# A fused two-block transformer kernel: the shared expert in plain fp32, all 64 experts routed, a new order of units

## The chip, the core and the metric

The kernel runs on one core of one Trainium2 chip. The metric is the device time of one execution in microseconds. A core has five engines with an instruction queue each: TensorE (PE, matmuls; its weight loads are listed as PEld), VectorE (DVE), ScalarE (ACT), GpSimd (POOL) and SyncE (SP). SP computes nothing here; its queue issues nearly all transfers from HBM. Each queue is executed in order, so an instruction that waits holds back all behind it on that engine.

## What is computed

Two blocks over 256 tokens of width 1024, in fp32. The change is in the mixture of experts of the first block:

```python
def moe_ffn(h, router_w, router_bias, w_gate, w_up, w_down, sh_gate, sh_up, sh_down):
    scores = jax.nn.sigmoid(hf @ router_w)               # 256 x 64
    # top 2 of each group of 8 -> best 4 of 8 groups -> best 8 experts of a token
    gate = gate / jnp.sum(gate, axis=-1, keepdims=True) * ROUTED_SCALE
    ...
    def expert_block(xb, e):
        return (jax.nn.silu(xb @ w_gate[e]) * (xb @ w_up[e])) @ w_down[e]
    routed = ...   # sum over each token's 8 experts, times its gate
    shared = (jax.nn.silu(hf @ sh_gate) * (hf @ sh_up)) @ sh_down
    return routed + shared
```

Every expert has three matrices of 1024 x 256 fp32 (gate, up, down), 1 MiB each. All 64 experts are read, whatever the tokens choose.

## The kernel before

The program runs six stages one after the other: the mixer of the first block (`first_mixer`), `moe`, and four stages of the second block. Weights come through one class, `Weights`: a plan lists all loads of the program in the order of use, `issue` puts a load on SP's queue whenever a buffer of 1 MiB is free, `next` hands out the next one and frees those used before. There are four buffers of tag `w`; a stage may lend more through `extra` (tags `a8`, `h2`). Weights marked for it are split into a high and a low fp32r part, `wh` by ACT (line 218) and `wl` by DVE or POOL (line 224), and then multiplied in three fp32r matmuls for each chunk (lines 289 to 291, or 325 to 327). Unmarked ones are used as they are, in plain fp32.

`moe` first normalises the mixer's output into `xn`, transposes it into `h_f` (`transpose_mod`) and splits that into `h_hi` and `h_lo`. The router (`router`, a generator) is interleaved with matmuls: each `yield from wait(W1)` and so on lets so many calls of `fast` pass, which stand between other matmuls. It scores the tokens, selects eight experts each, counts the tokens of each expert, ranks the experts by count, and writes the expert numbers by rank to `K.ids` (`r_ids`). Only then can SP load an expert's weights, since the address of a load (`rank_ap`) comes from `r_ids`; up to then SP can load only what does not depend on the routing.

Two sets of weights don't: the shared expert (item `("s",)`) and, as expert 0 is computed for all tokens without being ranked (`N_STATIC = 1`, item `("e", 0)`), that expert. Both are computed from split weights. The other 63 are taken by rank. The two busiest are computed for all 256 tokens ("dense", 3 loads). The others are packed into units of 128 token slots: one expert of 128 slots, 96 + 32, 64 + 64, or four of 32 (3, 6, 6 and 12 loads). A unit gathers its tokens (line 1481; one gather serves two units), multiplies gate and up (line 1500), is transposed, multiplies down (line 1531) and scatters the result into four PSUM banks (line 1543). `ORDER` is a table written by hand that sets the order of units and dense experts, and with it the order of loads: a unit's gate and up loads, then the down loads of the unit ahead of it.

If an expert has more tokens than its slots, `fallback` (line 1696) recomputes what is missing in a loop over all 64 experts. Its branch stands after item 1 and is passed by all engines; after it SP waits until all transfers issued so far have landed (line 1700), since both ways of the branch meet there.

Of the kernel before, what the change touches and what calls it, by code (L numbers as in the profile page):

```python
# [16 lines left out]
P = 128  # L17
# [456 lines left out]
def transpose_mod(K, xn, scale, shift, name, mid):  # L474
    nc = K.nc
    full = a8(K, name + "_f", tag="hf", bufs=1)
    hi, lo = a8r(K, name, tag="h2", bufs=2)
# [66 lines left out]
def plan_mix(I):  # L544
# [35 lines left out]
    for j in range(4):  # L580
# [4 lines left out]
W1, W2, W3, W4 = 13, 3, 3, 4  # L585
N_STATIC = 1
N_DENSE = 2
WHOLE, MIXED, HALVES, QUARTERS = (128,), (96, 32), (64, 64), (32,) * 4
DENSE = "dense"
ORDER = [WHOLE, HALVES, QUARTERS, MIXED, DENSE, QUARTERS, HALVES, DENSE, HALVES, MIXED, QUARTERS, WHOLE, HALVES,  # L590
         HALVES, QUARTERS, MIXED, QUARTERS, HALVES, HALVES, MIXED, QUARTERS, HALVES, HALVES, MIXED, QUARTERS, HALVES,
         WHOLE]
# [14 lines left out]
def _items():  # L607
    units = [Unit(o) for o in ORDER if o != DENSE]
# [7 lines left out]
    assert len(caps) == N_EXP - N_STATIC  # L616
# [8 lines left out]
    out = [("s",)] + [("e", e) for e in range(N_STATIC)]  # L625
# [17 lines left out]
def plan_moe(I):  # L643
    pl = []
    wg, wu, wd = I["w_gate"][0], I["w_up"][0], I["w_down"][0]

    def dense(gate, up, down):
        for w in (gate, up):
            pl.append((one(w.rearrange("(p k) f -> p k f", k=KC), (KC, D_EXP)), True))
        return [(one(down.rearrange("(k p) d -> p k d", p=P), (2, D)), lambda K: K.g2)]  # L650
# [12 lines left out]

    pend = []
    for it in ITEMS:
        if it[0] == "d":
            pl.extend(rows(w, it[1]) for w in (wg, wu))
        elif it[0] == "u":
            pl.extend(rows(w, r) for w in (wg, wu) for r in it[1].ranks)
        else:  # L670
            ws = [I[f"sh_{n}"][0] for n in ("gate", "up", "down")] if it[0] == "s" else [w[it[1]] for w in (wg, wu, wd)]
            nxt = dense(*ws)
        pl.extend(pend)
        if it[0] == "d":
            pend = [down(it[1])]
        elif it[0] == "u":
            pend = [down(r) for r in it[1].ranks]
        else:
            pend = nxt
    pl.extend(pend)  # L680
    return pl
# [429 lines left out]
def first_mixer(K, x, _):  # L1111
# [185 lines left out]
    inv_std(K, K.mo[1])  # L1297
# [3 lines left out]
def router(K, h_full, rw, rb, M):  # L1301
# [58 lines left out]
    nc.vector.scalar_tensor_tensor(ec[:, 2:3], ec[:, 1:2], M.kmul, M.kadd, op0=OP.mult, op1=OP.add)  # L1360
    nc.vector.reciprocal(tot, tot)
    for tt in range(TT):
        nc.vector.tensor_scalar(s[:, tt], s[:, tt], tot[:, tt:tt + 1], 2.5, op0=OP.mult, op1=OP.mult)
# [10 lines left out]
    pt = psum(K)  # L1374
    for i, src in enumerate((sel, s)):
        for tt in range(TT):
            nc.tensor.transpose(pt[:N_EXP, i * T + tt * P:i * T + tt * P + P], src[:, tt], K.ident)
# [6 lines left out]
    nc.vector.tensor_copy(K.ids, pi[0:1, :N_EXP])  # L1384
    nc.vector.tensor_copy(sg.rearrange("p a b -> p (a b)"), pt[:N_EXP])
# [9 lines left out]
    nc.vector.tensor_scalar(M.flag, om, 0.0, None, op0=OP.is_gt)  # L1395
    yield from wait(W4)
# [39 lines left out]
def dense_split(K, a, bufs=1):  # L1436
# [3 lines left out]
    return tuple(q.rearrange("p (a b) -> p a b", a=2) for q in (ah, al))  # L1440

# [105 lines left out]
def moe(K, x, _):  # L1547
# [8 lines left out]
    xn = a8(K, "xn", (TT, D))  # L1556
# [35 lines left out]
    K.W.flush()

    def mid(hf):
        if K.fast is None:
            K.fast = router(K, hf, rw, rb, M)
        fast(K)

    hh, hl, hf = transpose_mod(K, xn, K.mod[:, 3], K.mod[:, 2], "h2", mid)
    for tt in range(TT):  # L1600
        nc.scalar.activation(M.xn[0][:, tt], xn[:, tt], AF.Copy)
    g2 = K.g2 = wk.tile([P, D], F32, name="g2b", bufs=1)
    mod_bcast(K, K.mrow, 5, g2)
    K.W.extra = [("a8", 4, 4)]
    K.pool_sub = 1
    outs = [psum(K) for _ in range(4)]
    prev = scat = ahead = None
    for n, it in enumerate(ITEMS + [None]):
# [9 lines left out]
        else:  # L1618
            h = hf if it[0] == "d" else (hh, hl)
            pg = dense_proj(K, h)  # L1620
        if it == ("e", 0):
            for _ in K.fast:
                pass
            K.fast = None
            for tt in range(TT):
                nc.vector.tensor_sub(M.xn[1][:, tt], xn[:, tt], f32(M.xn[0][:, tt]))
            K.pool_sub = 3
        if prev is not None:
# [3 lines left out]
            else:  # L1632
                if pit[0] == "e":
                    dense_gate(K, act, (K.ident[:N_EXP, pit[1]:pit[1] + 1], M.sg[:, 1]))
                elif pit[0] == "d":
                    dense_gate(K, act, (M.perm[:, pit[1]:pit[1] + 1], M.sg[:, 1]))
                act = act.rearrange("p (a b) -> p a b", a=2) if pit[0] == "d" else dense_split(K, act)
# [3 lines left out]
        if n + 1 < len(ITEMS) and ITEMS[n + 1][0] == "u" and ITEMS[n + 1][2] == 0:  # L1641
            G = wk.tile([P, TT, T], F32R, name="u_G")
            pair = ITEMS[n + 1][3]
            sel = [unit_sel(K, u, M, G, P * q) for q, u in enumerate(pair)]
            xg_next = gather(K, G, M, P * len(pair))
            ahead = [unit_route(K, gg) for gg in sel], xg_next
# [5 lines left out]
        else:  # L1652
            cur = (it, dense_act(K, pg, dense_proj(K, h)))
        if it == ("e", 0):
            for tt in range(TT):
                nc.scalar.activation(x[:, tt], x[:, tt], AF.Copy, scale=ALPHA)
# [1055 lines left out]
```

## Time and profile before

| what | value |
|---|---|
| median of 3 runs (lowest to highest) | 1844.7 us (1844.55 to 1847.16) |
| the profiled execution: its time, its span | 1845.26 us, 1843.4 us |
| mean granted clock of TensorE | 0.977 |
| PE, DVE, ACT, POOL busy | 1710.4, 1001.1, 741.7, 450.3 us |
| read from HBM over the span | 400.04 MB |
| PE, share of the chain that ended last | 45% |
| DMA, share of that chain | 10% |

The profile is of one execution, in microseconds from the span's start. Busy shares are means over stages with different limits; the stage that the change touches lies between about 460 and 1035 us. A plain fp32 matmul shows as two records in the trace, so `x32` there are 16 matmuls of the program.

### The profile page before, as it was taken

How to read it: one execution, taken by the hardware profiler on the slowest of the kernel's cores; microseconds unless marked ns; L12 is line 12 of the kernel's file. 1: busy time of each engine (PE TensorE's matmuls, PEld its weight loads, DVE VectorE, ACT ScalarE, POOL GpSimd, SP SyncE). 2: the span in 40 equal slices, each digit the busy share in tenths (PEclk: the TensorE clock that was granted, in tenths of full speed). 3: DMA queues.
4: the chain of work that ended last, by engine and by line, in shares of the span. 5: the costliest groups of instructions: out<-in, count | busy, mean ns of one | idle time of the engine just before them, and what ended most of it. 6: DMA issues, size and time to landing. Idle time of an engine off the chain costs nothing.

```text
span 1843.4 us, 35420 instructions
## 1 busy us (share of the span) xinstructions
PE 1710.4 (93%) x14701; PEld 1397.0 (76%) x14701; DVE 1001.1 (54%) x1744; ACT 741.7 (40%) x1263; POOL 450.3 (24%) x331
## 2 busy tenths in 40 slices
PE   7999999998789999988898899999988889989999
PEld 5999988897674665544454588899978877779998
DVE  4764666557742223323332576744479967864444
ACT  3554666544421111211121354544447555544443
POOL 2232332224600110000000223223335533332222
PEclk9999999999799999999999999999999999999999
DMA  9666666554358998999999544465524300026552
GB/s 312 206 193 219 216 206 201 181 181 162 127 228 354 380 384 345 421 420 420 420 421 420 171 137 138 139 206 193 180 84 160 121 24 3 25 93 205 177 189 92
DMA packets 182711, 403.40 MB, mean 219 GB/s; under 512 B 12352, under 2 KB 140716, under 8 KB 155796
## 3 DMA queue, kind: packets, MB, share of 16 engines
q1 hardware_dynamic: 181700, 398.73, 59.6%
q8 instruction: 116, 1.90, 0.4%
q0 software_dynamic: 848, 2.38, 0.4%
q14 instruction: 47, 0.39, 0.1%
HBM read 400.04 MB, written 1.05 MB: 218 GB/s over the span
## 4 chain that ended last, share of the span: by engine, by line
PE 45%; DMA 10%; DVE 9%; issue 3%; ACT 2%; POOL 1%; SPq 0%; DVEq 0%; ACTq 0%; POOLq 0%
PE ps L1500 6%; DMA w<-in_w_gate_dram 5%; PE ps L290 5%; PE ps L289 5%; PE ps L291 5%; PE ps L1531 3%; DMA w<-in_w_down_dram 3%; PE ps L325 3%; PE ps L327 3%; PE ps L326 3%; PE ps L1481 2%; DMA w<-in_w_up_dram 2%; PE ps L1413 2%; DVE tmx L2123 1%; DVE wl L224 1%
## 5 line engine op out<-in xcount | busy, mean ns | idle before, releaser
L224 DVE TENSOR_TENSOR wl<-w,wh 128x1024 fp32r<-128x1024 f32 x220 | 334.3, 1533 | 179.0 <-ACT wh L218 178.6
L289 PE MATMUL ps<-hT_hi,wh 128*128 128x256 f32 (+1 forms) x1488 | 428.3, 288 | 0.0
L291 PE MATMUL ps<-hT_hi,wl 128*128 128x256 f32 (+1 forms) x1488 | 421.4, 283 | 1.9 <-POOL wl L224 1.1
L290 PE MATMUL ps<-hT_lo,wh 128*128 128x256 f32 (+1 forms) x1488 | 422.1, 284 | 1.0 <-DVE hT_lo L465 1.0
L224 POOL TENSOR_TENSOR wl<-w,wh 128x1024 fp32r<-128x1024 f32 x112 | 280.3, 2504 | 555.7 <-ACT wh L218 547.6
L218 ACT ACTIVATE wh<-w 128x1024 fp32r<-128x1024 f32 (+1 forms) x332 | 340.6, 1050 | 144.7 <-PE ps L290 96.1
L289 PEld LDWEIGHTS ps<-hT_hi,wh 128*128 128x128 f32 (+1 forms) x1488 | 284.6, 191 | 6.3 <-issue 3.8
L290 PEld LDWEIGHTS ps<-hT_lo,wh 128*128 128x128 f32 (+1 forms) x1488 | 284.8, 191 | 4.3 <-DVE hT_lo L465 3.0
L291 PEld LDWEIGHTS ps<-hT_hi,wl 128*128 128x128 f32 (+1 forms) x1488 | 284.7, 191 | 2.6 <-POOL wl L224 1.5
L1500 PE MATMUL ps<-w,xg 128*32 128x256 f32 (+2 forms) x2272 | 201.7, 393 | 24.0 <-DMA w<-in_w_gate_dram 12.8
L1500 PEld LDWEIGHTS ps<-w,xg 128*32 128x32 f32 (+2 forms) x2272 | 114.6, 124 | 113.9 <-issue 24.3
L1531 PE MATMUL ps<-w,u_aT 128*32 128x512 f32 (+2 forms) x568 | 103.1, 608 | 7.3 <-DMA w<-in_w_down_dram 7.2
L1507 ACT ACTIVATE u_s<-ps 128x256 f32<-128x256 f32 x25 | 9.6, 383 | 182.5 <-PE ps L1500 182.5
L1490 ACT ACTIVATE xg<-ps,modc 128x256 f32<-128x256 f32 (+1 forms) x52 | 28.9, 556 | 129.7 <-PE ps L1481 129.7
L1034 POOL DMA_DIRECT2D lngb<-in_ln_g_dram x2 | 1.3, 636 | 326.0 <-PE ps L1481 326.0
L499 ACT ACTIVATE u_yh<-res_t 128x512 fp32r<-128x512 f32 x50 | 31.5, 630 | 122.0 <-DVE res_t L1534 122.0
L1531 PEld LDWEIGHTS ps<-w,u_aT 128*32 128x32 f32 (+2 forms) x568 | 29.7, 122 | 66.2 <-issue 46.3
L1508 DVE SCALAR_TENSOR_TENSOR u_s<-u_s,u_gate,ps 128x256 f32<-128x256 f32 x25 | 12.0, 481 | 124.7 <-ACT u_s L1507 124.7
L325 PE MATMUL ps<-wh,e_ah 128*128 128x512 f32 x192 | 75.2, 392 | 0.0
L326 PE MATMUL ps<-wl,e_ah 128*128 128x512 f32 x192 | 75.2, 391 | 0.0
L327 PE MATMUL ps<-wh,e_al 128*128 128x512 f32 x192 | 74.8, 390 | 0.0
L1481 PE MATMUL ps<-u_G,xn_hi 128*128 128x256 f32 (+1 forms) x208 | 55.8, 304 | 12.6 <-DVE u_G L1451 12.6
(600 smaller groups left out, 3267.0 us busy)
## 6 DMA issues: line engine op xcount, KB each, us to landing
w<-in_w_gate_dram SPq DMA_DIRECT2D x64, 1024.0 KB, 16.6
w<-in_w_up_dram SPq DMA_DIRECT2D x64, 1024.0 KB, 14.0
w<-in_w_down_dram SPq DMA_DIRECT2D x64, 1024.0 KB, 15.7
w<-in_w_in_dram SPq DMA_DIRECT2D x36, 1024.0 KB, 5.3
w<-in_ffn_w_gate_dram SPq DMA_DIRECT2D x22, 1024.0 KB, 5.4
w<-in_ffn_w_up_dram SPq DMA_DIRECT2D x22, 1024.0 KB, 5.3
w<-in_ffn_w_down_dram SPq DMA_DIRECT2D x22, 1024.0 KB, 4.8
w<-in_w_ada_dram SPq DMA_DIRECT2D x16, 1024.0 KB, 7.8
```

Of the source, the lines that this page charges most:

```text
L218: nc.scalar.activation(h[:rows, :n], v, AF.Copy)
L224: eng.tensor_sub(l[:rows, :n], v, f32(h[:rows, :n]))
L289: mm(out, wh, xh[:, kc], start=kc == 0, stop=False)
L290: mm(out, wh, xl[:, kc], start=False, stop=False)
L291: mm(out, wl, xh[:, kc], start=False, stop=kc == nk - 1)
L325: mm(o, xh[:, xk + kc, ts], wh, start=first and kc == 0, stop=False)
L326: mm(o, xh[:, xk + kc, ts], wl, start=False, stop=False)
L327: mm(o, xl[:, xk + kc, ts], wh, start=False, stop=last and kc == nk - 1)
L1413: K.nc.tensor.matmul(o[:, i * T:i * T + T], w[1][0][:, kc, i::2], h[:, kc], start=kc == 0, stop=kc == KC - 1)
L1481: nc.tensor.matmul(o, src[:, tt, kc * P:kc * P + P], G[:, tt, :n], start=tt + i == 0, stop=tt + i == 2)
L1500: K.nc.tensor.matmul(gu[c:c + m, cs], xg[kc // 4][:, kc % 4, off + c:off + c + m], ts[j][:, kc], start=kc == 0, stop=kc == KC - 1, tile_po ...
L1531: nc.tensor.matmul(y[c0:c0 + m], aT[:, c, c0:c0 + m], ts[j][:, c, hf * 512:hf * 512 + 512], start=c == 0, stop=c == 1, tile_position=(0, c0))
```

## The change

The shared expert's weights are no longer split, nor is `h_f`; it is computed in plain fp32, its down weights are multiplied by `g2` on POOL ahead of the router (`dense_scale`), and the router's steps are placed between its matmuls. Expert 0 is ranked as the other 63. Two buffers of tag `h2` are lent from the start of the stage, and all ten from the end of the router. The first half of `xn` is written by DVE, no longer by ACT. `ORDER` is new: 25 units and two dense experts as before, one unit of 64 + 32 + 32 slots in place of one of 64 + 64, four experts first and last. The branch of `fallback` stands after the first unit.

```diff
-W1, W2, W3, W4 = 13, 3, 3, 4
-N_STATIC = 1
+W1, W2, W3, W4 = 18, 4, 3, 6
 N_DENSE = 2
-ORDER = [WHOLE, HALVES, QUARTERS, MIXED, DENSE, QUARTERS, HALVES, DENSE, HALVES, MIXED, QUARTERS, WHOLE, HALVES,
+KINDS = {"W": (128,), "M": (96, 32), "H": (64, 64), "T": (64, 32, 32), "Q": (32,) * 4}
+ORDER = "QWHMHQWWQHTHHQMHdQHdQMMMHHQ"
...
+    for nm in ("gate", "up"):
+        pl.append((one(I[f"sh_{nm}"][0].rearrange("(p k) f -> p k f", k=KC), (KC, D_EXP)), False))
+    pl.append((one(I["sh_down"][0].rearrange("(p k) d -> p k d", k=2), (2, D)), False))
...
-    for kc in range(KC):
-        nc.scalar.activation(hi[:, kc], full[:, kc], AF.Copy)
-        (nc.gpsimd if kc in (2, 4, 6, 7) else nc.vector).tensor_sub(lo[:, kc], full[:, kc], f32(hi[:, kc]))
-        if kc in (1, 5, 7):
-            mid(full)
-    return hi, lo, full
+    return full
...
             K.nc.tensor.matmul(o[:, i * T:i * T + T], w[1][0][:, kc, i::2], h[:, kc],
                                start=kc == 0, stop=kc == KC - 1)
+            fast(K)
...
+def dense_scale(K, w):
+    for c in range(2):
+        K.nc.gpsimd.tensor_mul(w[:, c], w[:, c], K.g2)
...
+    K.W.extra = [("a8", 3, 4), ("h2", 2, 2)]
+    K.W.issue()
+    mod_bcast(K, K.mrow, 5, g2)
...
+    nc.vector.tensor_scalar(xk[:, 0], xs[:, 0], mo[3], mo[4], op0=OP.mult, op1=OP.add)
+    inv_std(K, mo)
+    dense_scale(K, K.W.raw[K.W.i + 2][1][0])
...
+    hf = transpose_mod(K, xn, K.mod[:, 3], K.mod[:, 2], "h2")
+    K.fast = router(K, hf, rw, rb, M)
+    for _ in range(3):
+        fast(K)
...
+    act = dense_act(K, dense_proj(K, hf), dense_proj(K, hf))
+    for _ in K.fast:
+        pass
+    K.W.extra = [("a8", 4, 4), ("h2", 2, 2)]
+    dense_down(K, outs, K.W.next()[1][0], act, True)
+    ahead = route(ITEMS[0][3])
...
-        if n == N_STATIC:
+        if n == 0:
             fallback(K, x, hf, g2, M)
-            K.W.extra = [("a8", 4, 4), ("h2", 2, 2)]
```

PE's queue from the router's scores on, before: after scores (`rw`), `id` and a broadcast come split matmuls of the shared expert (`wh`, `wl`), 39 of them ahead of the counts (`ones<-r_br`); the ids are the rows of `r_pm`. The first and the last rows of the stretch up to the counts:

```order
L1307 MATMUL ps<-h_f,rw 64x256 x8
L1314 MATMUL ps<-id_5171,r_st 128x64 x2
L796 MATMUL ps<-mrow,ident 128x512 x2
L289 MATMUL ps<-h_hi,wh 128x256
L290 MATMUL ps<-h_lo,wh 128x256
...
L291 MATMUL ps<-h_hi,wl 128x256
L1356 MATMUL ps<-ones,r_br 64x1 x2
```

The same place of PE's queue in the change, up to the shared expert's down matmuls (line 1434):

```order
L1285 MATMUL ps<-h_f,rw 64x256 x8
L1292 MATMUL ps<-id_5174,r_st 128x64 x2
L1393 MATMUL ps<-h_f,w 128x256 x18
L1334 MATMUL ps<-ones,r_br 64x1 x2
L1393 MATMUL ps<-h_f,w 128x256 x4
L1342 MATMUL ps<-ident,r_ec 64x64
L1393 MATMUL ps<-h_f,w 128x256 x3
L1355 MATMUL ps<-r_pm,r_ec 1x64
L1356 MATMUL ps<-r_pm,r_ec 1x64
...
L1393 MATMUL ps<-h_f,w 128x256
L1434 MATMUL ps<-w,e_a 128x512 x8
```

What stood between the scores and the ids was 39 split matmuls to the counts and more behind them; now it is 25 plain ones in all, and the shared expert ends a few matmuls after the ids.

POOL's queue between the end of the mixer (`mo`) and the branch, before:

```order
L1054 TENSOR_TENSOR mo<-mo 128x1
L1558 IOTA iota_5156 128x128
L1560 IOTA iota_5158 64x64
...
L1574 TENSOR_TENSOR id_5171<-ident 128x64
...
L224 TENSOR_TENSOR wl<-w,wh 128x1024
L492 TENSOR_TENSOR h_lo<-h_f,h_hi 128x256 x4
L224 TENSOR_TENSOR wl<-w,wh 128x1024 x6
L216 TENSOR_TENSOR w<-w,g2b 128x1024 x2
```

and in the change:

```order
L1033 TENSOR_TENSOR mo<-mo 128x1
L1426 TENSOR_TENSOR w<-w,g2b 128x1024 x2
L1566 IOTA iota_5166 128x128
L1568 IOTA iota_5168 64x64
L1571 IOTA ecol 64x1
...
L1575 TENSOR_TENSOR id_5174<-ident 128x64
```

The subtractions of the splits are gone from POOL, and two multiplications by `g2` have moved ahead of `id`, which the router's second matmul reads.

SP's queue of loads from the first one that needs the ids to the branch, before (`r_flag` is read at the branch):

```order
L183 DMA w<-in_w_gate_dram 128x2048
...
L183 DMA w<-in_w_up_dram 128x2048
L183 DMA w<-in_w_down_dram 128x2x1024
...
L183 DMA w<-in_w_down_dram 128x2048
...
L183 DMA w<-in_w_gate_dram 128x2048
...
L1699 TENSOR_LOAD r_flag
```

Eight routed loads and expert 0's down (`128x2x1024`) stand there. In the change there are fourteen routed ones: the first unit's four gates and four ups, the second unit's gate and up, and the first unit's four downs. The last rows ahead of the branch:

```order
L183 DMA w<-in_w_gate_dram 128x2048
...
L183 DMA w<-in_w_up_dram 128x2048
...
L183 DMA w<-in_w_down_dram 128x2048
...
L1673 TENSOR_LOAD r_flag
```

## Rows read from the trace of the kernel before

**Rows 1.** Windows: window, length, PE, PEld, DVE, ACT, POOL busy, clock, DMA share, GB/s.

```profile
494.00:500.00 6.00, 6.00 (x43) 5.71 (x42) 2.15 (x7) 0.86 (x1) 0.00 (x0) 0.82 0.71 251
500.00:510.00 10.00, 6.28 (x53) 6.08 (x52) 9.31 (x5) 0.83 (x2) 9.02 (x3) 0.99 1.00 402
510.00:540.00 30.00, 28.55 (x153) 25.20 (x154) 14.37 (x24) 10.49 (x17) 0.00 (x0) 0.89 0.39 139
540.00:580.00 40.00, 37.26 (x341) 23.03 (x340) 12.52 (x30) 6.38 (x14) 0.00 (x0) 0.96 0.85 338
580.00:600.00 20.00, 17.12 (x126) 8.07 (x122) 3.58 (x6) 1.64 (x3) 0.00 (x0) 0.91 1.01 422
600.00:720.00 120.00, 115.02 (x862) 73.55 (x864) 32.64 (x75) 16.82 (x38) 9.39 (x4) 1.00 0.91 362
720.00:1010.00 290.00, 260.43 (x2254) 148.05 (x2250) 92.81 (x210) 48.87 (x108) 1.17 (x2) 0.98 1.01 421
```

**Rows 2.** Timeline of SP's queue: start, length, what.

```profile
494.68 0.36 SPq L183 DMA_DIRECT2D w<-in_w_gate_dram  x1
...
531.86 8.69 SPq L183 DMA_DIRECT2D w<-in_w_gate_dram  x4
```

**Rows 3.** Waits of SP's queue, 526 to 545: total, times, longest.

```profile
SPq L1700 <- SPq L1700: 3.7, 2, 3.2
```

**Rows 4.** Timeline of DVE in the router: start, length, instruction, idle before.

```profile
478.05 0.29 DVE L1341 TENSOR_TENSOR r_bm<-r_b,r_kp 128x128 f32<-128x128 f32 x1
478.38 2.48 DVE L1342 TENSOR_TENSOR r_bm<-r_bm,r_kn 128x128 f32<-128x128 f32 x1
...
481.93 1.27 DVE L1349 TENSOR_TENSOR r_br<-r_br,r_bm 128x128 f32<-128x128 f32 x1
483.24 2.34 DVE L1351 TENSOR_TENSOR r_s<-r_s,r_br 128x128 f32<-128x128 f32 x1
...
486.13 1.68 DVE L1360 SCALAR_TENSOR_TENSOR r_ec<-r_ec,kmul,kadd 64x1 f32<-64x1 f32 x1
...
487.91 2.42 DVE L1363 TENSOR_SCALAR r_s<-r_s,r_tot 128x64 f32<-128x64 f32 x2
...
493.33 0.21 DVE L1384 CAST r_ids<-ps 1x64 int32<-1x64 f32 x1 [2.28 <-PE ps L1382]
```

**Rows 5.** Timeline of POOL around the router.

```profile
464.75 0.19 POOL L1054 TENSOR_TENSOR mo<-mo 128x1 f32<-128x1 f32 x1
...
467.10 0.31 POOL L1574 TENSOR_TENSOR id<-ident 128x64 f32<-128x64 f32 x1
...
478.33 11.79 POOL L224 TENSOR_TENSOR wl<-w,wh 128x1024 fp32r<-128x1024 f32 x5 [2.28 <-ACT wh L218]
...
502.63 6.66 POOL L216 TENSOR_TENSOR w<-w,g2b 128x1024 f32<-128x1024 f32 x2
```

**Rows 6.** Timeline of PE in the router.

```profile
472.59 0.63 PE L1314 MATMUL ps<-id,r_st 128*128 128x64 f32 x4 [0.56 <-ACT r_st L1310]
...
483.36 0.55 PE L1356 MATMUL ps<-ones,r_br 128*64 128x1 f32 x4 [3.74 <-DVE r_br L1349]
```

**Rows 7.** Windows, as in rows 1: a stretch of the router.

```profile
482.00:486.00 4.00, 2.65 (x13) 2.49 (x13) 3.93 (x5) 0.39 (x1) 4.00 (x3) 0.56 0.00 0
```

**Rows 8.** Chain that ended last, 529 to 760: start, length, work.

```profile
597.12 7.11 PE ps L1413 x32
...
688.61 7.06 PE ps L1666 x16
...
713.74 3.59 PE ps L1500 x64
...
745.28 3.60 PE ps L1500 x32
```

**Rows 9.** Windows, as in rows 1: where the stream of expert weights ends.

```profile
1016.00:1018.00 2.00, 2.00 (x12) 1.64 (x11) 0.42 (x1) 0.00 (x0) 0.00 (x0) 1.00 0.98 362
```

**Rows 10.** Timeline of PE: the last unit's down matmuls.

```profile
1028.96 3.60 PE L1531 MATMUL ps<-w,u_aT 128*128 128x512 f32 x8
```

More of the change, by code (lines that the diff above doesn't have):

```diff
@@ L607, in _items @@
 def _items():
-    units = [Unit(o) for o in ORDER if o != DENSE]
+    units = [Unit(KINDS[o]) for o in ORDER if o != DENSE]
     caps = [T] * N_DENSE
@@ L624, in _items @@
         groups[-1].append(units.pop(0))
-    out = [("s",)] + [("e", e) for e in range(N_STATIC)]
+    out = []
     for i, g in enumerate(groups):
@@ L662, in down @@
         return (dyn(wd, r, "a (p k) d -> p (a k) d", (2, D), k=2), False)
+    for nm in ("gate", "up"):
+        pl.append((one(I[f"sh_{nm}"][0].rearrange("(p k) f -> p k f", k=KC), (KC, D_EXP)), False))
+    pl.append((one(I["sh_down"][0].rearrange("(p k) d -> p k d", k=2), (2, D)), False))
     pend = []
     for it in ITEMS:
[L666 to L672, printed above, removed]
-        pl.extend(pend)
[L674 to L679, printed above, removed]
+        ranks = [it[1]] if it[0] == "d" else it[1].ranks
+        pl.extend(rows(w, r) for w in (wg, wu) for r in ranks)
+        pl.extend(pend)
+        pend = [down(r) for r in ranks]
     pl.extend(pend)
@@ L1359, in router @@
     nc.vector.tensor_copy(ec[:, 1:2], pc[:N_EXP, 0:1])
[L1360 to L1363, printed above, removed]
+    nc.vector.tensor_scalar(ec[:, 2:3], pc[:N_EXP, 0:1], float(N_EXP), M.ecol, op0=OP.mult, op1=OP.subtract)
     yield from wait(W2)
@@ L1384, in router @@
     nc.vector.tensor_copy(K.ids, pi[0:1, :N_EXP])
+    pt = psum(K)
+    for i, src in enumerate((sel, s)):
+        for tt in range(TT):
+            nc.tensor.transpose(pt[:N_EXP, i * T + tt * P:i * T + tt * P + P], src[:, tt], K.ident)
     nc.vector.tensor_copy(sg.rearrange("p a b -> p (a b)"), pt[:N_EXP])
@@ L1395, in router @@
     nc.vector.tensor_scalar(M.flag, om, 0.0, None, op0=OP.is_gt)
+    for tt in range(TT):
+        nc.vector.tensor_sub(M.xn[1][:, tt], M.x[:, tt], f32(M.xn[0][:, tt]))
     yield from wait(W4)
@@ L1440, in dense_split, with dense_down @@
     return tuple(q.rearrange("p (a b) -> p a b", a=2) for q in (ah, al))
+def dense_scale(K, w):
+    for c in range(2):
+        K.nc.gpsimd.tensor_mul(w[:, c], w[:, c], K.g2)
+def dense_down(K, outs, w, a, first=False):
+    a = a.rearrange("p (a b) -> p a b", a=2)
+    for c in range(2):
+        for tt in range(TT):
+            for q in range(2):
+                K.nc.tensor.matmul(outs[2 * tt + q], a[:, c, tt * P:tt * P + P], w[:, c, q * 512:q * 512 + 512],
+                                   start=first and c == 0, stop=False)
 def unit_sel(K, u, M, G, off):
@@ L1618, in moe @@
         else:
[L1619 to L1627, printed above, removed]
+            pg = dense_proj(K, hf)
         if prev is not None:
@@ L1641, in moe @@
         if n + 1 < len(ITEMS) and ITEMS[n + 1][0] == "u" and ITEMS[n + 1][2] == 0:
[L1642 to L1646, printed above, removed]
+            ahead = route(ITEMS[n + 1][3])
         if it is None:
@@ L1652, in moe @@
         else:
[L1653 to L1656, printed above, removed]
+            cur = (it, dense_act(K, pg, dense_proj(K, hf)))
         if prev is not None:
```

84 lines of the change are left out of this document (27 added, 57 removed).

## The prediction, made before the change was run

> **What bounds the kernel now.** I began with the windows of the stage, whose last column is what HBM delivers. From 720 to 1010 it is 421 GB/s with the DMA engines fully busy, while PE is busy 260 of 290 us [rows 1]. So this long part is bound by the stream of expert weights: a load of 1.0486 MB takes 1.0486 / 421 = 2.49 us, and whatever PE saves there is worth nothing. The stream can't begin before the expert numbers are known. DVE writes them at 493.33 [rows 4] and SP issues the first routed load at 494.68 [rows 2]. From there 63 x 3 loads and expert 0's down, 190 in all, need 190 x 2.49 = 473 us, which would end at 968. The stream ends at about 1018 [rows 9]. The 50 us between are the stops of the stream: each window's length times what its rate lacks to 421 is 2.4, 0.4, 20.1, 7.9, 0 and 16.8 us, 47.6 in all, nothing behind 720 [rows 1]. About one load that belongs to no expert fills the rest. Then PE is behind: the last unit's down matmuls start at 1028.96 [rows 10], 11 us after the last weights.
>
> The stage is therefore head (up to the first routed load) + number of loads x 2.49 + stops + tail. Each edit is priced by which of these four it moves.
>
> **Head.** Three things set the ids' time now. PE's matmul of scores and `id` starts at 472.59 [rows 6]. DVE then selects; some of its operations cost far more than their shape: 0.29 us for one, 2.48 for the next with the same shape, then 1.27 and 2.34 [rows 4], in a stretch in which POOL subtracts splits, 11.79 / 5 = 2.36 us each [rows 5]. PE waits 3.74 us for the result and begins the counts at 483.36 [rows 6]. Last, PE runs from 482 to 486 at a mean clock of 0.56, close to its lower level of 1.2 GHz [rows 7], with the split matmuls around.
>
> In the change no POOL instruction stands beside the selection. Held against 0.29, the two stretched operations ahead of the counts' input (2.48, 1.27) lose 3.2 us; the three behind (2.34, 1.68 on 64x1, and 2.42 for two) lose about 5 [rows 4]. But `id`, now ready at 467.41 [rows 5], comes behind the two multiplications by `g2`. They begin where POOL ends `mo` (464.94) [rows 5] and take 2 x 2.36 = 4.7 us if they cost what the subtractions of the same shape cost, or 6.66 if they cost what the same two cost later on [rows 5]; with the iotas ahead of `id` (467.10 − 464.94 − what is dropped, about 1.5) `id` is ready at 471.2 to 473.1. So the matmul at 472.59 stays where it is within a microsecond. Its queue then holds 18 plain matmuls up to the counts. One takes 7.11 / 16 = 0.444 us (two records are a matmul) [rows 8], so 18 take 8.0 and the counts start at about 481.2. DVE's selection, which ends at 483.20 now, is ready by 480.0 without the 3.2, so it no longer sets the time. From the counts to the ids (10 us now, 483.36 to 493.33) stand 7 matmuls (3.1) and short steps of 0.2 us or so each [rows 4], five of them and their hand-overs 1.4: ids at 485.7, first routed load 1.2 later at 486.9. That is **−7.8 us**. Bounds: −10 if PE's 18 matmuls partly run ahead of `id`, and 0 if PE stays at 1.2 GHz, where 25 matmuls cost 25 x 0.444 = 11.1 more and eat it.
>
> The shared expert's loads depend on nothing routed and land before the router, so the two lent buffers cost no wait. The writing of `xn` on DVE, the moved subtractions for `xn2` and the scaling of x lie under the shared expert's matmuls and the first weights' landing; if that cover is missing, they delay the first unit, not the stream, which has ten buffers.
>
> **Loads.** Expert 0 is routed, and its gate and up, which came under the router, now come behind the ids: 192 loads instead of 190, **+5.0 us**. No bound is needed: both are counted in the program.
>
> **Stops.** This is the largest term. Now, at the ids, five of the stage's buffers are held by expert 0 and the shared expert, which are still being computed. The first routed loads fill what is free and then SP is stopped: 139 GB/s from 510 to 540 [rows 1]. At 531.86 SP takes up loading [rows 2], behind a wait at the branch of 3.7 us [rows 3]. Then PE is late: it computes expert 0's rest and the first units one after the other, while loads come at once, and the stream stops again for 7.9 and 16.8 us up to 720, through the second dense expert (688.61) [rows 1, 8].
>
> In the change the shared expert ends about when the ids come. Two loads are issued at 487, six more when its two projections are through at 491, two more behind: ten loads are 25 us of stream, up to 512. The first unit's gates, four loads, land at 497 and its ups at 507, so PE begins it at about 505 and gives back the first buffers at about 509, before the ten have landed. Then the branch: SP again waits for all that it issued, 3.7 us as now [rows 3], of which the landing queue covers a part; I take 3.
>
> Behind it, what matters is how far PE lags behind the stream. A unit costs PE 15.8 us (two units from 713.74 to 745.28, with half a gather) [rows 8], a dense expert 3 x 7.1 = 21.3 [rows 8]. The stream gives 12 loads or 29.9 us for a unit of four experts, 22.4 for one of three, 14.9 for two, 7.5 for one or for a dense expert. So PE gains 14 on a unit of four, 6.6 on one of three, loses 0.9 on one of two, 8.3 on one of a single expert and 13.8 on a dense one. Added up along the new table from a first lag of 17 us (stream at 488, first unit at 505), the lag never rises above that first value: a unit of four comes first, and ones of a single expert or dense experts are followed by one soon. Added up along the old table it starts late, from seven loads that landed before 531 and units of one and two behind them, and climbs by 13.8 at each dense expert; the stops of rows 1 lie there. So I take off both of the stops at 510 to 580, but for the 3 at the branch, and leave 10 us, 40% of the 24.7 between 540 and 720, since a buffer is held beyond its first use and my ledger knows only means: 13 us are left, **−34.6**. Bounds: 3 left (−44.6), the branch alone; or 28 left (−19.6), as if all 24.7 stayed.
>
> **Tail.** The last unit is one of four, with its downs landing last, 2.49 us apart, against 3.60 for eight matmuls [rows 10]. PE should wait for the last load and start its matmuls, 0.9 us, right behind it, instead of 11 us later: **−10.5**. Bounds: −11, and 0 if PE's lag at the end is as large as now.
>
> **Sum.** −7.8 + 5.0 − 34.6 − 10.5 = −47.9. The profiled execution took 1845.3 (1.9 outside its span), 0.6 over the median of 1844.7: 1845.3 − 47.9 = 1797.4, say **1797**. All best bounds give −60.6 (1785), all worst −14.6 (1831).
>
> **A rule that speaks against it.** The rows show DVE operations with two operands stretched from 0.29 to 2.48 us, about one POOL subtraction, while POOL works [rows 4, 5]. The Trainium skill, "SBUF — State Buffer", section "Who interferes with whom", says that such DVE instructions and POOL instructions that read SBUF exclude each other for the whole of an instruction. The trace agrees (0.29 against 2.48). By it the multiplications, beside DVE's writing of `xn` half by half, could be held up like that, and the sum would be 2.4 to 4.7 higher (the first rival); without it, as summed.
>
> **Rivals.**
> - *POOL is late with `id`* (0.08). The multiplications and DVE's `xn` exclude each other in turn, one or two times 2.36 [rows 5] on the path to the scores: +2.4 to 4.7, 1801. For it: those stretched rows. Against: POOL has its two instructions in hand when DVE is still at the norm.
> - *PE at 1.2 GHz in the router* (0.08). PE idles before the scores and then has the clock of 0.56 seen now [rows 7]; 25 plain matmuls cost 11 us more, partly under DVE's work: −7.8 becomes 0, 1805. Against: no stop of PE ahead of the counts any more.
> - *The order saves nothing* (0.13). The first dozen loads come sooner, but PE's lag builds up elsewhere, and stops of 30 us stay, as units of four want eight buffers at a time: 1845.3 − 7.8 + 5.0 − 17.6 − 10.5 = 1814. For it: ten buffers are fewer than the twelve loads of such a unit. Against: these come at the rate of the stream and not of PE.
> - *Slower: the fallback runs* (0.02). A rank that had 64 slots now has 32. With the given inputs the expert there has 28 tokens, so four to spare; from 33 on the loop over 64 experts is run, 64 x 3 x 2.49 = 478 us more. Between there is nothing: the term is 0 or 478.
> - *No change* (0.02). If the head's gain is eaten (0), the tail stays (0), and of 47.6 stops 42 remain, the sum is +5.0 − 5.6, about nothing. For this PE, not the stream, would have to bound all of 510 to 720; the 25 units and 2 dense experts are 438 us by the prices above, 40 less than 192 loads.
>
> **How the numbers follow.** The forecast has 0.67. The first three rivals lie between 1801 and 1814 and are within the range; its low end, 1787, is 10 under the forecast (the 10 us of stops that I left standing), its high end, 1817, the third rival with 3 to spare. What is left out is both ends of the sum, the fallback and no change. A measurement can tell 0.2%, 3.7 us, from no change: faster 0.96, same 0.02, slower 0.02.
>
> **What would show it.** Head: the first routed load at 487, the counts at 481, DVE's selection without operations over 1 us. If `id` ends after 473, the first rival; if the clock is near 0.5 from 472 to 486, the second. Loads: 192 at 2.49 us. Stops: the windows behind the branch at 421 GB/s; a window from 540 to 720 under 390 would be the third rival. Tail: down matmuls of the last unit within 3 us of the last load, and the stage's end near 987. The prediction is wrong above all if PE's unit of four costs more than 15.8 us, as it was read from units of other kinds: the ledger then has less to spare.

## The result, and the profile after

The changed kernel takes 1803.2 us (median of 4 runs, 1802.7 to 1805.1) against 1844.6: a ratio of 0.9776, 95% interval 0.9759 to 0.9793, 41.4 us faster. The forecast was 1797, with a range from 1787 to 1817. The profiled execution took 1802.7, its span is 1800.9.

The windows of the stage after the change, with the columns of [rows 1]:

```profile
520.00:530.00 10.00, 9.93 (x72) 7.60 (x74) 3.64 (x9) 3.49 (x9) 0.00 (x0) 1.00 0.65 247
540.00:600.00 60.00, 56.28 (x520) 32.75 (x516) 21.72 (x48) 12.09 (x27) 0.00 (x0) 1.00 1.01 420
600.00:720.00 120.00, 112.08 (x835) 68.60 (x834) 40.69 (x92) 20.72 (x46) 0.00 (x0) 0.99 1.01 421
790.00:800.00 10.00, 9.42 (x51) 8.14 (x50) 2.48 (x6) 2.93 (x8) 0.00 (x0) 1.00 0.89 369
800.00:810.00 10.00, 10.00 (x95) 4.78 (x94) 4.05 (x6) 1.26 (x2) 0.66 (x1) 1.00 0.85 298
850.00:860.00 10.00, 10.00 (x53) 6.55 (x55) 1.88 (x3) 0.63 (x1) 0.00 (x0) 1.00 0.82 320
860.00:870.00 10.00, 10.00 (x139) 5.77 (x132) 2.18 (x4) 0.89 (x2) 3.84 (x2) 1.00 0.94 367
890.00:900.00 10.00, 10.00 (x146) 5.29 (x148) 4.43 (x9) 3.07 (x9) 0.00 (x0) 1.00 0.83 325
```

From 540 to 790 the stream runs at 420 to 421 GB/s; the stops of [rows 1] between 540 and 720 are gone. Two places are left: the branch at 520 to 530, and 790 to 900, where PE is busy nearly all the time and the stream waits for it. There each dense expert holds its buffers over a gather. On PE the first one's gate and up (line 1393) are 7.6 us apart, and the gather of the next two units stands between them. SP gets one buffer at the end of the gate, at 785.44, and the next at the end of the up, at 800.21; the row of its queue spans these two issues alone:

```profile
778.23 7.18 PE L1393 MATMUL ps<-h_f,w 128*128 128x256 f32 x32
...
793.00 7.18 PE L1393 MATMUL ps<-h_f,w 128*128 128x256 f32 x32 [0.50 <-DVE xg L1482]
```

```profile
785.44 15.10 SPq L183 DMA_DIRECT2D w<-in_w_up_dram  x2
```

The router on DVE (start, length, work), with the selection that was stretched in [rows 4]:

```profile
474.91 0.28 DVE L1319 TENSOR_TENSOR r_bm<-r_b,r_kp 128x128 f32<-128x128 f32 x1
475.23 0.29 DVE L1320 TENSOR_TENSOR r_bm<-r_bm,r_kn 128x128 f32<-128x128 f32 x1
...
476.60 0.29 DVE L1327 TENSOR_TENSOR r_br<-r_br,r_bm 128x128 f32<-128x128 f32 x1
476.92 0.29 DVE L1329 TENSOR_TENSOR r_s<-r_s,r_br 128x128 f32<-128x128 f32 x1
...
483.87 0.21 DVE L1358 CAST r_ids<-ps 1x64 int32<-1x64 f32 x1 [0.48 <-PE ps L1356]
```

On POOL ahead of it, the two multiplications and `id`:

```profile
463.82 5.08 POOL L1426 TENSOR_TENSOR w<-w,g2b 128x1024 f32<-128x1024 f32 x2 [0.23 <-issue]
...
469.53 0.31 POOL L1575 TENSOR_TENSOR id<-ident 128x64 f32<-128x64 f32 x1
```

On PE from the scores to the first unit, and at the end of the stage:

```profile
466.89 3.56 PE L1285 MATMUL ps<-h_f,rw 128*64 128x256 f32 x16
471.05 0.63 PE L1292 MATMUL ps<-id,r_st 128*128 128x64 f32 x4 [0.60 <-ACT r_st L1288]
471.51 8.00 PE L1393 MATMUL ps<-h_f,w 128*128 128x256 f32 x36
479.44 0.39 PE L1334 MATMUL ps<-ones,r_br 128*64 128x1 f32 x4
...
490.15 8.83 PE L1434 MATMUL ps<-w,e_a 128*128 128x512 f32 x16 [1.49 <-DVE e_a L1402]
...
503.13 4.09 PE L1495 MATMUL ps<-w,xg 128*32 128x256 f32 x70
...
984.12 1.06 PE L1526 MATMUL ps<-w,u_aT 128*32 128x512 f32 x6
986.21 3.62 PE L1526 MATMUL ps<-w,u_aT 128*32 128x512 f32 x26 [1.03 <-DMA w<-in_w_down_dram]
```

SP's queue has its first routed load at 485.22, and issues nothing between 508.83 and 524.53. At the branch (line 1674) it waits 14.1 us in all (total, times, longest), against 3.7 before [rows 3]; the loads still in flight cover most of that. At the end of the stage it issues the next stage's loads (`in_hy_w_in`) from 976.32 on:

```profile
485.22 4.94 SPq L183 DMA_DIRECT2D w<-in_w_gate_dram  x4
...
506.80 2.03 SPq L183 DMA_DIRECT2D w<-in_w_down_dram  x4
524.53 1.53 SPq L183 DMA_DIRECT2D w<-in_w_gate_dram  x2
...
976.32 13.69 SPq L183 DMA_DIRECT2D w<-in_hy_w_in_dram  x4
```

```profile
SPq L1674 <- SPq L1674: 14.1, 7, 2.8
```

For this kernel and those below the same account was drawn up from each trace. Stops are summed from the first routed load on in steps of 2 us, each step's length times what its rate lacks to 421 GB/s, until the bytes of all expert loads and of one 1.05 MB load more (the next norm's parameters) are through; there the stream ends. The bytes of other loads in flight are counted with them. The tail runs from there to the end of the last unit's down matmuls. The last column is that end less the start of the scores' matmuls (466.89 in the change, 469.59 before).

| kernel | first routed load | loads x 2.49 | stops | stream's end | tail | scores to last down |
|---|---|---|---|---|---|---|
| before | 494.7 | 473 | 47.9 | 1018.3 | 14.3 | 563.0 |
| change | 485.2 | 478 | 16.5 | 982.4 | 7.4 | 522.9 |
| before, new order | 493.8 | 473 | 28.1 | 997.6 | 7.6 | 536.7 |
| change, old order | 487.4 | 478 | 24.6 | 992.7 | 13.9 | 537.7 |
| change, expert 0 static | 485.5 | 473 | 27.3 | 988.6 | 7.7 | 529.1 |
| change, POOL beside the selection | 490.9 | 478 | 17.0 | 988.6 | 7.7 | 532.2 |
| change, ids early | 481.3 | 478 | 16.7 | 978.7 | 7.6 | 518.7 |
| change, ids late | 488.3 | 478 | 15.8 | 984.7 | 8.2 | 526.0 |
| change, no early buffers | 486.4 | 478 | 16.1 | 983.2 | 7.9 | 523.2 |
| change, no branch | 484.9 | 478 | 11.4 | 977.0 | 7.6 | 518.0 |
| change, late branch | 484.9 | 478 | 11.5 | 977.1 | 8.5 | 519.1 |
| ids early, dense apart | 482.0 | 478 | 14.3 | 977.0 | 4.9 | 514.1 |
| ids early, late branch, third order | 481.3 | 478 | 11.7 | 973.6 | 6.9 | 513.4 |
| change, last downs by expert | 485.7 | 478 | 15.9 | 982.3 | 10.0 | 525.0 |

The last column is the one to compare: the program's last stage, whose code is the same everywhere, took between 480.9 and 488.8 us in these executions (from its first `tmx` to the span's end), and the scores began between 464.1 and 468.9 in kernels that don't differ up to there. So totals can't separate less than some 5 us here.

### The profile page after: what moved, and what is told of

Its sections match the earlier page's. It is cut to its first block, busy times and chain, and to the rows that moved or that the text cites. A ratio compares the mean times of both kernels' runs of the same rounds, so it can differ in the third digit from the quotient of the medians.

```text
span 1800.9 us, 35213 instructions
## 1 busy us (share of the span) xinstructions
PE 1683.3 (93%) x14619; PEld 1370.3 (76%) x14619; DVE 975.6 (54%) x1738; ACT 724.5 (40%) x1239; POOL 428.2 (24%) x316
## 3 DMA queue, kind: packets, MB, share of 16 engines
HBM read 400.04 MB, written 1.05 MB: 223 GB/s over the span
## 4 chain that ended last, share of the span: by engine, by line
PE 46%; DMA 9%; DVE 9%; issue 3%; ACT 2%; POOL 1%; SPq 0%; DVEq 0%; ACTq 0%; POOLq 0%
PE ps L1495 6%; PE ps L290 6%; PE ps L289 6%; PE ps L291 6%; DMA w<-in_w_gate_dram 5%; PE ps L1526 3%; DMA w<-in_w_down_dram 3%; PE ps L325 3%; PE ps L327 3%; PE ps L326 3%; PE ps L1476 2%; PE ps L1393 2%; PE ps L1538 1%; DVE wl L224 1%; DVE tmx L2097 1%
## 5 line engine op out<-in xcount | busy, mean ns | idle before, releaser
L224 DVE TENSOR_TENSOR wl<-w,wh 128x1024 fp32r<-128x1024 f32 (+2 forms) x215 | 328.9, 1544 | 171.8 <-ACT wh L218 171.3
L224 POOL TENSOR_TENSOR wl<-w,wh 128x1024 fp32r<-128x1024 f32 (+1 forms) x105 | 264.0, 2514 | 540.9 <-ACT wh L218 537.0
L218 ACT ACTIVATE wh<-w 128x1024 fp32r<-128x1024 f32 (+1 forms) x320 | 328.4, 1050 | 130.0 <-PE ps L290 84.6
L1495 PE MATMUL ps<-w,xg 128*32 128x256 f32 (+2 forms) x2336 | 197.1, 388 | 21.1 <-DMA w<-in_w_gate_dram 14.4
L1426 POOL TENSOR_TENSOR w<-w,g2b 128x1024 f32<-128x1024 f32 x6 | 14.5, 2430 | 391.5 <-DMA w<-in_w_down_dram 391.2
L1526 PE MATMUL ps<-w,u_aT 128*32 128x512 f32 (+2 forms) x584 | 98.7, 596 | 6.0 <-DMA w<-in_w_down_dram 6.0
L326 PE MATMUL ps<-wl,e_ah 128*128 128x512 f32 x176 | 68.8, 391 | 0.0
L325 PE MATMUL ps<-wh,e_ah 128*128 128x512 f32 x176 | 68.7, 391 | 0.0
L327 PE MATMUL ps<-wh,e_al 128*128 128x512 f32 x176 | 68.5, 389 | 0.0
## 6 DMA issues: line engine op xcount, KB each, us to landing
w<-in_w_gate_dram SPq DMA_DIRECT2D x64, 1024.0 KB, 16.1
w<-in_w_down_dram SPq DMA_DIRECT2D x64, 1024.0 KB, 14.8
```

Of the source, the lines that this page charges most:

```text
L218: nc.scalar.activation(h[:rows, :n], v, AF.Copy)
L224: eng.tensor_sub(l[:rows, :n], v, f32(h[:rows, :n]))
L325: mm(o, xh[:, xk + kc, ts], wh, start=first and kc == 0, stop=False)
L326: mm(o, xh[:, xk + kc, ts], wl, start=False, stop=False)
L327: mm(o, xl[:, xk + kc, ts], wh, start=False, stop=last and kc == nk - 1)
L1495: K.nc.tensor.matmul(gu[c:c + m, cs], xg[kc // 4][:, kc % 4, off + c:off + c + m], ts[j][:, kc], start=kc == 0, stop=kc == KC - 1, tile_po ...
```

## The experiments

**The order alone, both ways.** The old table in the changed kernel, and the new one in the kernel before:

```diff
-ORDER = "QWHMHQWWQHTHHQMHdQHdQMMMHHQ"
+ORDER = "WHQMdQHdHMQWHTQMQHHMQHHMQHW"
```

> The change with the table of units of before (one unit of 64 + 64 replaced by 64 + 32 + 32, so that 64 experts fit); all else as in the change. Theory (order): PE's lag builds up again behind the early dense experts and the stream stops between 540 and 720; stops grow from 16.5 to about 32, the last unit is one of 128 slots, total about 1819. Rival (the stops came only from the late ids and expert 0 ahead of the units): the order is worth nothing, 1803 within 3.

Measured: 1821.5 (1817.1 to 1828.1); the stage 14.8 us longer, 8.1 by stops and 6.5 by the tail. The stops are back between 600 and 720, as expected, but grow to 24.6 and not to 32:

```profile
600.00:720.00 120.00, 114.32 (x850) 71.21 (x850) 36.21 (x88) 18.00 (x41) 4.67 (x2) 1.00 0.94 378
```

> The kernel before with the table of units of the change alone (63 ranked, 64 + 64 in place of 64 + 32 + 32). Theory (the order's worth, 15 us in the run with the old order, doesn't need the early start): the stage is 10 to 18 us shorter than 563.0, total 1827 to 1835. Rival (the order only helps once the shared expert and expert 0 are out of PE's way, since its lag at the start is otherwise far above what the order can take back): less than 5 us, 1840 to 1845.

Measured: 1821.5 (1815.6 to 1825.1), a ratio to before of 0.9886 (0.9871 to 0.9901); the stage 26.3 us shorter, more than both theories said. The stop at 510 to 540 falls from 20.1 to 12.0, the one at 600 to 720 is gone, and 8.1 are lost at 720 to 900 instead, where before lost none:

```profile
510.00:540.00 30.00, 25.50 (x238) 19.60 (x238) 12.56 (x16) 10.39 (x17) 2.50 (x1) 0.99 0.65 252
540.00:580.00 40.00, 37.31 (x266) 25.37 (x264) 12.52 (x30) 6.39 (x14) 0.00 (x0) 0.96 0.91 372
...
600.00:720.00 120.00, 117.63 (x907) 76.21 (x908) 44.83 (x99) 24.30 (x54) 0.00 (x0) 1.00 1.01 421
720.00:900.00 180.00, 166.73 (x1294) 98.85 (x1290) 49.24 (x115) 23.15 (x49) 9.44 (x4) 0.98 0.98 402
```

So the order is worth about as much as everything else together. Alone it gives 26.3; everything else alone (the old order in the change) gives 563.0 − 537.7 = 25.3; together they give 40.1, as both remove some of the same stops (19.8 and 23.3 alone, 31.4 together).

**Expert 0 ahead of the units again.** It is computed from weights that come under the router, its matmuls stand between the shared expert and the first unit, and 63 are ranked:

```diff
-    out = []
+    out = [("e", e) for e in range(N_STATIC)]
...
+        if it[0] == "e":
+            for q in (wg, wu):
+                pl.append((one(q[it[1]].rearrange("(p k) f -> p k f", k=KC), (KC, D_EXP)), False))
+            pend = [(one(wd[it[1]].rearrange("(p k) d -> p k d", k=2), (2, D)), False)]
+            continue
```

> The change with expert 0 computed for all tokens again, in plain fp32, from weights that come under the router, ahead of the units (63 ranked; the unit of 64 + 32 + 32 is one of 64 + 64). Theory (PE's time ahead of the first unit is what stops the stream): two loads less behind the ids give 5.0 back, but the first unit starts about 21 us later, with ten buffers of 25 us between; stops of 16.5 grow to 30 or 40, total 1811 to 1822. Rival (only the number of loads counts, PE catches up): 1798.

Measured: 1809.2 (1806.0 to 1811.6), the stage 6.2 longer. The two loads less give 5.0 back and the stops take 10.8 more: from 510 to 520 nearly nothing is read, and SP issues no load between 506.6 and 518.4, while PE computes expert 0; the gather of the first units stands between its gate and its up here too.

```profile
510.00:520.00 10.00, 9.42 (x68) 7.46 (x70) 2.19 (x5) 1.89 (x6) 4.67 (x2) 1.00 0.16 56
520.00:540.00 20.00, 17.18 (x140) 9.48 (x128) 3.52 (x12) 0.39 (x1) 0.00 (x0) 1.00 0.97 397
540.00:600.00 60.00, 59.44 (x529) 36.05 (x529) 22.25 (x47) 12.79 (x28) 0.00 (x0) 1.00 0.94 388
```

```profile
506.22 0.34 SPq L183 DMA_DIRECT2D w<-in_w_down_dram  x1
518.42 0.34 SPq L183 DMA_DIRECT2D w<-in_w_gate_dram  x1
```

The direction is the theory's; its 30 to 40 us of stops were 27, and the total lies under its range.

**POOL at work beside DVE's selection.** The low part of `xn` is subtracted on POOL, three times over, and no longer on DVE:

```diff
-    for tt in range(TT):
-        nc.vector.tensor_sub(M.xn[1][:, tt], M.x[:, tt], f32(M.xn[0][:, tt]))
...
         nc.scalar.activation(M.xn[0][:, tt], xn[:, tt], AF.Copy)
+    for _ in range(3):
+        for tt in range(TT):
+            nc.gpsimd.tensor_sub(M.xn[1][:, tt], xn[:, tt], f32(M.xn[0][:, tt]))
```

> The change with the two subtractions for the low part of xn taken from DVE and given to POOL, right behind ACT's rounding, three times over: six POOL instructions of 128x1024 beside DVE's selection, 2.4 us each or more. Theory (the two shut each other out): DVE operations with two operands that took 0.29 us take about 2.4 again, the input of the counts is ready 5 us later (482 instead of 476.9), PE waits for it 2 to 3 us, ids 3 us later or more, total 1805 to 1808. Rival (the stretched operations of before came from something else, as the split's hand-overs): they stay at 0.29, ids unchanged, total 1803 or less, since DVE is rid of 2.3 us.

Measured: 1815.0 (1810.7 to 1821.6). POOL's six, DVE beside them, and PE's counts with the clock behind them:

```profile
470.37 14.12 POOL L1590 TENSOR_TENSOR xn_lo<-xn,xn_hi 128x1024 fp32r<-128x1024 f32 x6 [2.90 <-ACT xn_hi L1587]
```

```profile
475.10 2.27 DVE L1315 TENSOR_SCALAR r_kn<-r_kp 128x16 f32<-128x16 f32 x1
477.29 0.28 DVE L1319 TENSOR_TENSOR r_bm<-r_b,r_kp 128x128 f32<-128x128 f32 x1
477.61 2.33 DVE L1320 TENSOR_TENSOR r_bm<-r_bm,r_kn 128x128 f32<-128x128 f32 x1
...
481.00 1.28 DVE L1327 TENSOR_TENSOR r_br<-r_br,r_bm 128x128 f32<-128x128 f32 x1
482.32 2.32 DVE L1329 TENSOR_TENSOR r_s<-r_s,r_br 128x128 f32<-128x128 f32 x1
...
489.54 0.21 DVE L1358 CAST r_ids<-ps 1x64 int32<-1x64 f32 x1 [1.08 <-PE ps L1356]
```

```profile
482.43 0.56 PE L1334 MATMUL ps<-ones,r_br 128*64 128x1 f32 x4 [5.56 <-DVE r_br L1327]
```

```profile
482.40:486.60 4.20, 4.17 (x12) 3.02 (x12) 2.77 (x5) 0.00 (x0) 2.08 (x1) 0.50 0.00 0
```

Three of the four operations of 0.28 to 0.29 us take 1.28 to 2.33 again; one that has 16 elements per partition takes 2.27, against 0.17 in the change, about one POOL instruction (14.12 / 6 = 2.35). From the scores' start to the ids it is 489.54 − 464.12 = 25.4 us, against 17.0 in the change and 23.7 before. The stage is 9.2 longer. So work on POOL beside the selection costs 8.4 us, more than the 6.7 that this stretch had gained, and more than the 3 foreseen. It comes in two parts. The counts start 5.8 later (18.3 us behind the scores instead of 12.6), as small operations further ahead in the selection are hit as well. From there to the ids it is 7.1 us instead of 4.4: PE has waited 5.56 us, and the granted clock of its next matmuls is 0.50, where it was 1.00 in the change.

**The ids earlier and later.** Only the places of the router's steps between the plain matmuls:

```diff
-W1, W2, W3, W4 = 18, 4, 3, 6
+W1, W2, W3, W4 = 12, 1, 2, 8
```

> The change with the router's steps placed after 12, 1, 2 and 8 plain matmuls instead of 18, 4, 3 and 6. Both theories: expert numbers 4 us earlier than 483.9. Prediction's account (head, stops and tail add up): the stream ends 4 us earlier, 1799. Rival (ten buffers are full before the first unit frees any, since the first unit doesn't start earlier): most of the 4 us comes back as a stop around 507 to 525, total down by 1.5 at most, 1801.5 to 1803.

Measured: 1799.2 (1796.4 to 1800.7), the stage 4.2 shorter, the stops unchanged at 16.7. The rival fails: its premise that the first unit doesn't start earlier is wrong. DVE's subtraction for `xn` (2.34 us, from 486.83 in the change, from 482.88 here) moves ahead with the router, PE pauses 0.85 us instead of 1.49 before the shared expert's down matmuls, and these take 7.13 instead of 8.83, at a granted clock of 1.00 from 490 to 500 instead of 0.83; the first unit begins at 501.17, 2.7 us earlier counted from the scores:

```profile
467.59 3.15 PE L1285 MATMUL ps<-h_f,rw 128*64 128x256 f32 x16
...
489.88 7.13 PE L1434 MATMUL ps<-w,e_a 128*128 128x512 f32 x16 [0.85 <-DVE e_a L1402]
...
501.17 7.85 PE L1495 MATMUL ps<-w,xg 128*32 128x256 f32 x128
```

With `W1` to `W4` = 26, 4, 2, 0:

> The change with the router's steps placed after 26, 4, 2 and 0 plain matmuls: the expert numbers come about 3.3 us later. Account of the prediction and its rival agree here: a later stream finds buffers free, so nothing hides it, +3.3, about 1806.5. Should it cost nothing, the ids don't set the start of the stream's end at all.

Measured: 1807.1 (1803.5 to 1809.6), the stage 3.1 longer. Between these two the stage follows the first routed load nearly one for one: counted from the scores, that load came 4.6 earlier and 3.1 later.

**The buffers lent early.**

```diff
-    K.W.extra = [("a8", 3, 4), ("h2", 2, 2)]
+    K.W.extra = [("a8", 3, 4)]
     K.W.issue()
```

> The change without the two h2 buffers lent at the start of the stage (both are lent from the end of the router as before). Both theories look at the same numbers: if the early buffers carry part of the gain, SP's first eight routed loads come in fewer and later groups and the first stop grows by 5 us or more; if not, since what SP loads ahead of the ids (the shared expert's three) fits into the four of tag w, the first loads and the stops are those of the change, 1803 within 3.

Measured in one execution: 1807.0, the stage 523.2 and the stops 16.1, both as in the change (the total's 4 us lie in the last stage, 486.6 against 483.4, and in the later scores). No gain of this part of the change is seen.

**The branch.** Left out first, and with it the recomputation of what overflows an expert's slots, which isn't needed with these inputs:

```diff
-        if n == 0:
-            fallback(K, x, hf, g2, M)
```

> The change without the branch to the fallback: the recomputation of what overflows an expert's slots is left out (nothing overflows with these inputs). Theory (the stop of 4.1 us at 520 to 530 is SP waiting at the branch for all that it issued): the stop is gone and 3 to 4 us come off the total, 1799 to 1800. Rival (the ten buffers are full there anyway): the stop stays, 1803.

Measured: 1796.6 (1794.9 to 1801.3); the stop at 520 to 530 is gone and the stage 4.9 shorter, more than the 3 to 4 foreseen:

```profile
520.00:530.00 10.00, 9.93 (x73) 6.94 (x75) 4.10 (x8) 3.77 (x10) 0.00 (x0) 1.00 1.01 420
```

Then kept, but after the last unit (`n == len(ITEMS) - 1`):

> The change with the branch to the fallback after the last unit's gate and up instead of after the first unit. Theory (SP's drain at the branch stops the stream wherever loads are still to come; behind the last load there is none left to stop): the stage is 4 to 5 us shorter as in the run without the branch, total 1797 to 1799, unless the next stage's first weights, which now wait for the drain, come too late. Rival (the drain only moves to the next stage's weights): what the stage gains the next one loses, 1803.

Measured: 1799.4 (1797.0 to 1804.1); the stage 3.9 shorter, and the next one's start is no later (30.5 us from the end of the last down to its matmuls of `blk` and `sq`, as in the change).

**What is left of the stops.** The ids early, and each dense expert between two units of four:

```diff
-ORDER = "QWHMHQWWQHTHHQMHdQHdQMMMHHQ"
+ORDER = "QdQMWTMHWQHWQHMHQHHMHHMHQdQ"
```

> The change with the router's steps after 12, 1, 2 and 8 matmuls (as in the run with the ids early, 1799) and an order in which each dense expert stands between two units of four: Q d Q M W T M H W Q H W Q H M H Q H H M H H M H Q d Q. Theory (what is left of the stops, 10 us at 790 to 900, is PE's lag at the two dense experts that stand close together): 3 to 6 us less than with the ids early alone, 1793 to 1796. Rival (the stops only move): 1799.

Measured: 1798.4 (1794.3 to 1800.2), the stage 4.6 shorter than with the ids early alone. The 9.9 us of stops at 790 to 900 are gone, but most of them are back elsewhere, 2.6 of them at 510 to 540 and 2.6 at 900 to 960:

```profile
510.00:540.00 30.00, 23.78 (x131) 19.04 (x134) 7.64 (x22) 4.25 (x11) 0.00 (x0) 0.94 0.81 324
790.00:900.00 110.00, 105.12 (x875) 61.17 (x865) 40.60 (x92) 20.79 (x45) 0.00 (x0) 1.00 1.01 420
900.00:960.00 60.00, 57.07 (x465) 36.92 (x463) 16.63 (x36) 9.42 (x21) 0.00 (x0) 0.97 0.98 402
```

All stops together fall by 2.4 only (16.7 to 14.3), so the rival is right for most of them; another 2.7 of the 4.6 lie in the tail. The total doesn't show the gain: this execution's last stage took 488.8 us, against 483.4 with the ids early alone.

> The router's steps after 12, 1, 2 and 8 matmuls, the branch after the last unit, and the order Q M H H H W Q H M M W Q H H M H T d Q H W Q M H Q d Q. Theory (ids, branch and PE's lag at the dense experts are separate terms and add up): stage from the scores to the last down 508 to 511 us against 522.9 in the change, total 1789 to 1794. Rival (with one stop gone another takes its place, since ten buffers are all there is): 514, as without the late branch, 1798.

Measured: 1790.6 (1789.1 to 1798.4), a ratio to before of 0.9719 (0.9700 to 0.9738), the lowest median. But its stage is 513.4, only 0.7 shorter than that of the version before it, which has the early branch and another order. The late branch alone gave 3.9, so the terms did not add up, as the rival said: 6.0 us of stops are back at 790 to 900. As two things differ between these versions, how much of that is the order and how much the branch stays open. Most of the lower total is a last stage of 481.9.

**The last unit's down matmuls.** Expert by expert instead of half by half over all four, for the last unit alone:

```diff
+    ys = [psum(K) for _ in range(2)] if last else None
+    if last:
+        for j, c0, m in u.tiles():
+            for hf in range(2):
+                for c in range(2):
+                    nc.tensor.matmul(ys[hf][c0:c0 + m], aT[:, c, c0:c0 + m], ts[j][:, c, hf * 512:hf * 512 + 512],
+                                     start=c == 0, stop=c == 1, tile_position=(0, c0))
...
```

> The change with the last unit's 16 down matmuls in the order of its four experts instead of half by half over all four. Theory (each expert's down was needed within the first four matmuls, so 13 of 16 stood behind the last load that lands): only about four matmuls stand behind it, the end of the last down comes 2 to 3 us earlier, stage from scores to that end 520 to 521 us against 522.9. Rival (the wait in front of them is not the last load's): no change, 522.9. The total can hardly tell 2 us.

Measured: 1807.5 (1803.8 to 1809.6), the stage 2.1 longer. The 16 matmuls take twice the time, without a wait for a load between them, so neither the theory nor its rival is tested:

```profile
983.43 8.86 PE L1527 MATMUL ps<-w,u_aT 128*32 128x512 f32 x32
```

## Why the prediction was right, and which terms were off

The account head + loads + stops + tail held, and the bound was named rightly; the sum was −47.9, the four measured terms add up to −42.8, and the span fell by 42.5. The earlier scores (below) helped by 2.7 that no term had foreseen.

- **Head: −7.8 forecast, −9.5 measured.** The scores began 2.7 us sooner, partly by chance (above); from there to the first routed load it is 18.3 instead of 25.1, −6.8. The 18 plain matmuls took the 8.0 forecast, the counts began at 479.44 and DVE's selection was ready at 476.89 without a stretched operation. From the scores to the counts it is 12.6 us instead of 13.8, from the counts to the ids 4.4 instead of 10.0. Behind the counts the stretched operations of [rows 4] (2.34, 1.68 and 2.42) became 0.29, 0.20 (another operation now) and 0.42, and PE, which no longer waits 3.74 us for DVE, keeps a granted clock of 1.00, where it had 0.56 [rows 7]. That POOL's work stretches the selection and brings the wait and the low clock with it is shown by putting it back; how much of the gain is due to fewer matmuls between the router's steps was not separated.
- **POOL late with `id` (rival): did not occur.** The multiplications took 5.08, `id` was ready at 469.84, and PE waited for ACT's `r_st` at 471.05 instead.
- **PE at 1.2 GHz in the router (rival): did not occur there.** The granted clock was 1.00 from 472 to 490. Only the scores themselves ran low, 3.56 us at 0.55 (467.0 to 470.5) against 2.44 before, where the clock was back at 1.00 from 469.5. It fell again, to 0.66 for 490 to 495, after PE's pause ahead of the shared expert's down matmuls.
- **Loads: +5.0, as counted.** Routing expert 0 is still a gain: 6.2 in the experiment, since the stops it avoids outweigh the loads.
- **Stops: −34.6 forecast, −31.4 measured (47.9 to 16.5).** The branch cost about 5 instead of 3 (11.4 without it): SP waited 14.1 us there and not "3.7 us as now", since five or six of the fourteen loads issued were still in flight by the rates, and these covered about 10 of it. The other part is the step "the lag never rises above that first value": at the two dense experts with two units between them, at 790 to 900, the stream stops for 10.1 us by the five windows shown. The ledger spread the gather over the units as a mean, but a whole one stands inside each dense expert, while its buffers are held. The reserve of 10 taken for the ledger's means was about that, but 2 more were lost until the first load's bytes flowed, for which the sum had left nothing.
- **Tail: −10.5 forecast, −6.9 measured.** The mechanism was right, PE waits for a down load at 986.21, but the term was mis-sized: I let 0.9 us of matmuls stand behind the last load, one expert's. The loop goes half by half over all four experts, so 26 of the 32 records stand behind it, 3.62 us. The six records ahead of the wait are three matmuls, one for each of the first three experts, so the wait is for the fourth's down, the last expert load in SP's queue. It lands at 986.2, 3.8 after the stream's end by the rates; the next stage's loads, issued from 976.32 on, are counted in these rates, and whether they also held the last load up was not tested. The term's own working doesn't close either: 11 us less ahead of the matmuls, and 0.9 behind the load in place of 3.60, would have been −13.7, further off. My own repair of the loop lost more than it could gain.
- **The order saves nothing (rival): refuted from both sides**, by 26.3 us in the kernel before and 14.8 in the change.
- **The fallback runs, or nothing changes (rivals): neither occurred**; the stream goes on at 311 GB/s and more from 525, without a loop of 478 us.

## What to carry to other kernels

When a stream of loads bounds a stage, add up its stops window by window, and ask at each which buffer comes free last: head, order and branch could each be priced before and after from that one column. Work that is taken off one engine may pay on another: the splits' removal paid on DVE, whose selection POOL had been holding up. Put what makes the bottleneck's consumer lag (here dense experts) next to what lets it catch up, and a full drain of the queue where nothing is left to stream; then count the stops of the whole stream again, as some only move. Measure a stage's gain inside the stage if a later one varies by more than the gain.

## What the runs showed of the hardware that was not expected

- A DVE `tensor_scalar` on 16 elements per partition took 2.27 us beside POOL's subtractions of 2.35, and 0.17 without them. The Trainium skill, "SBUF — State Buffer", section "Who interferes with whom", names `tensor_scalar` among the operations that can take the port pair shared with GpSimd, and says that whoever comes second is blocked for a whole instruction; these runs agree.
- Sixteen down matmuls of four experts with 32 tokens each took 4.68 us (1.06 + 3.62, without the wait between) when neighbours in the queue belong to different experts, that is to different quarters of the output, and 8.86 us in a row by expert, both at a granted clock of 1.00. The Trainium skill, "TensorEngine Tiling (Array Packing)", section "Key Properties", says that different tiles can execute matmuls in parallel; the trace agrees, by about a factor of two here.
